# A transformer layer on one core: w_down opens in its seven-product form instead of with four plain jobs

## The chip, the cores and the metric

The kernel runs on one core of one Trainium2 chip. The metric is device time in microseconds (us) of one execution, the median of several runs. Work is spread over TensorE (PE, matrix products), VectorE (DVE), ScalarE (ACT), GpSimd (POOL, which here mostly issues transfers) and SyncE (SP, which issues most loads). Each engine takes its own instructions strictly in the order in which the program lists them, and engines wait for one another by semaphores.

## The reference, cut to what matters

A hybrid encoder layer on a sequence of 512 tokens of width 2048. The part that the change touches is the last product of the feed-forward half:

```
h = rmsnorm(x, ffn_norm_w)
x = x + (silu(h @ w_gate) * (h @ w_up)) @ w_down     # w_gate, w_up: 2048 x 5632; w_down: 5632 x 2048
return rmsnorm(x, final_norm_w)
```

Ahead of it stand an RMSNorm, a projection `w_in`, dilated attention and gated linear attention, and the projection `w_out`. All data is fp32.

## The kernel before, in words

*Split products.* An fp32 operand is split into a high part (a cast to fp32r on ACT) and a low part (the difference, a subtraction on VectorE). A product is then three matmuls: high by high, high by low, low by high.

*Seven-product form.* A 2 x 2 block product is done with seven block products instead of eight, at the price of sums of blocks ahead of it and sums of products behind it (Strassen's way, in Winograd's form). The operands of the seven are called B11, B21, B22 (single blocks) and T1 to T4 (sums). The gate and up projections (`Feed`, "gate/up") are done so: 44 units, gate and up in turn, each of four pieces and with seven PSUM banks. `sums` makes the block sums of the weights on VectorE (L1493 to L1495), `split` the casts on ACT (L1506) and the differences on VectorE (L1511), `products` the matmuls (L1589, L1603). At a unit's end `evac7` empties its seven banks: nine copies on ACT (from L1629), adds on VectorE (L1623, L1624), and additions done by transfers that POOL issues (L1648 to L1655). `finish` applies the gate (SiLU, and the product of gate and up, L1697) and POOL stores the result to DRAM, `gd` (L1699).

*Pre-made sums.* VectorE has little to do in the w_out stage, so `ff.ahead()` makes there the block sums of 21 pieces of gate/up and stores them in DRAM; gate/up later only loads these (`self.pre`). They are the second piece of every other unit from the third on.

*w_down.* Its 44 tiles of 128 rows (k-tiles) are done in three parts. First come four plain jobs on k-tiles 0 to 3, one for each 512 columns: 4 half pieces of weights by 4 banks of 128 tokens by 3 matmuls each (L346 to L348). Their weights come through the stream `st` (loads L209, casts L237, differences L218), their operand from `gd` through `g_load` (L1816) and `g_split` (L1824 to L1828), and `evac_down` scales a bank on ACT and has POOL add it into `xd` in DRAM. Then `Down([[2, 4], [6, 8], [10, 12], [14, 16]])` does k-tiles 4 to 35 in the seven-product form. A number there names a duo: two tiles of `gd` (a "pair operand" each, two k-tiles), four k-tiles. A list of duos is a chunk, whose seven products stay in PSUM while its duos are added up; then they are copied out and added to partial products in DRAM, `md`. `run` takes steps in the order chunk, column half (C), product (ORDER), duo, 12 matmuls each (L2023 to L2025). Per step one block of weights (1024 elements per partition) is cast (L1991), and its difference taken (L1999), two steps ahead; T1, T3 and T2 first need a sum (L1976, L1979). `operands()` makes a pair operand from `gd`: load (L1917), four adds of 256 (L1931 to L1934), then casts and differences of four parts, B11 (256 wide), F2, T13 and T24 (512 wide; L1943 to L1947). It is a generator; `dn.make(n)` takes n steps of it. Last come four plain jobs on k-tiles 36 to 39 and a finish on 40 to 43.

*The hand-over.* During the last gate/up unit `down_start(q)` runs after each piece q. It loads the first operands of w_down and splits them. The first plain job makes Down's operands beside its matmuls (`before_down`).

*Order and buffers.* The order of the code is the order in every engine's queue. There are 8 PSUM banks (`ps`), 33 wide slots of SBUF (`b`, 1024 elements per partition) and 36 narrow ones (`a`, 512). A load is issued by SP in its turn, once its slot is free, and SP waits there until it is.

Of the kernel before, what the change touches and what calls it, by code (L numbers as in the profile page):

```python
# [36 lines left out]
KEEP_X, KEEP_F, MOST_4 = 5, 2, 13  # L37
# [81 lines left out]
def layer(nc, tc, x, attn_norm_w, w_in, rel_table, gw_f, gb_f, gw_b, gb_b, gla_norm_w, w_out,  # L119
# [7 lines left out]
    with tc.manual_schedule(), \  # L127
# [1389 lines left out]
        class Feed(Blocks):  # L1517
# [10 lines left out]
            def __init__(self):  # L1528
# [7 lines left out]
                    i for i, (u, q) in enumerate(seq) if u > 1 and q == 1 and u % 2 == 0)}  # L1536
# [295 lines left out]
        def down_start(q):  # L1832
            if q == 0:
                g_load(0)
            if q == 1:
                st.until = down_pieces
                st.limit = 3
                st.load()
                g_load(1)
            if q == 2:  # L1840
                g_split(0)
                st.split(down_first + 2)
            if q == 3:
                dn.make(1)
# [4 lines left out]

        def evac_down(c):  # L1850

            def f(banks):
                for t in range(4):
                    y = s2.get()
                    act.activation(y.t, banks[t].t, AF.Copy, scale=rstd2[:, t:t + 1])
                    put(banks[t])
                    pool.dma_start(out=xd[4 * c + t], in_=y.t, accum_op=OP.add)
                    put(y)
            return f

        def before_down(c):
            def f(i):
                if c == 0 and i == 0:
                    g_split(1)
                dn.make(1)
                if c == 2 and i >= 2 or c == 3:
                    dn.load()
                if c == 3 and i >= 2:
                    dn.prime(i - 2)
            return f  # L1870
# [6 lines left out]
        class Down:  # L1877

            ORDER = ((0, 1, "B11"), (6, 2, "T4"), (1, 3, "B21"), (3, None, "T1"), (4, None, "T3"), (2, None, "T2"),
# [4 lines left out]
            def __init__(self, chunks):  # L1884
# [14 lines left out]
            def load(self):  # L1899
                while self.todo and len(self.raw) < 8 and s4.free:  # L1900
# [7 lines left out]
            def operands(self):  # L1908
# [5 lines left out]
                def load():  # L1914
                    if qs and len(s4.free) > 1 and len(raws) < 2:
                        r = s4.get(F32, [P, 2, 512])
                        sp.dma_start(out=r.t.rearrange("p f t -> p (f t)"), in_=gd[qs[0]])  # L1917
                        raws.append((qs.popleft(), r))

                load()  # L1920
                load()
                yield
                while raws or qs:
                    load()
                    if not raws or len(s2.free) + 2 * (MOST_4 - state["big"]) < 9 + 1 or len(s2.free) < 4:
                        yield
                        continue
                    q, r = raws.popleft()
# [5 lines left out]
                    tt(t24.t[:, z], t24.t[:, a], f2[:, a], op=OP.subtract)  # L1934
                    yield
                    todo, slots = [], {}
                    for name, src, n in (("B11", n1[:, a], 256), ("F2", f2, 512), ("T13", t13.t, 512),
                                         ("T24", t24.t, 512)):
                        slots[name], hi, lo, hf = half_split(src, n)
                        todo.append((src, hi, lo, hf))  # L1940
                    for i, (src, hi, lo, hf) in enumerate(todo):
                        if i == 0:
                            act.activation(hi, src, AF.Copy, scale=-1.0)  # L1943
                            dve.scalar_tensor_tensor(lo, src, -1.0, hf, op0=OP.mult, op1=OP.subtract)
                        else:
                            act.copy(hi, src)
                            tt(lo, src, hf, op=OP.subtract)  # L1947
                        if i:
                            put((r, t13, t24)[i - 1])
                        if i == 1:  # L1950
                            load()
                        if i % 2:
                            yield
                    (_, b1h, b1l, _), (_, f2h, f2l, _), (_, t13h, t13l, _), (_, t24h, t24l, _) = todo
                    self.x[q] = dict(slots=slots, B11=(b1h, b1l), B21=(f2h[:, a], f2l[:, a]),
                                     B22=(f2h[:, z], f2l[:, z]), T1=(t13h[:, a], t13l[:, a]),
                                     T3=(t13h[:, z], t13l[:, z]), T2=(t24h[:, a], t24l[:, a]),
                                     T4=(t24h[:, z], t24l[:, z]))
# [154 lines left out]
            def run(self):  # L2113
                n_last = len(self.seq) - 14
                for i, (ch, C, k, d) in enumerate(self.seq):
# [16 lines left out]
                    while q not in self.x or q + 1 not in self.x:  # L2132
                        self.make(1)
# [4 lines left out]
                    if i % 14 in (0, 1, 2, 5, 11, 12, 13):  # L2138
                        self.make(1)
# [46 lines left out]
        down_first = len(st.halves)  # L2186
        for c in range(4):
            j = job("B", [piece512(w_down, c * 512, k) for k in (0, 2)], list(range(4)),
                    lambda k: gT[k], evac_down(c), before=before_down(c))
            if c == 3:  # L2190
                j.drop = drop_g
# [151 lines left out]
```

## Time and profile before

| | |
|---|---|
| median of 3 runs | 2139.51 us (2138.58 to 2139.54) |
| the profiled execution | 2140.3 us, its span 2138.5 us, granted TensorE clock 0.999 |
| PE matmul, busy | 2126.0 us, 99% of the span |
| DVE busy | 1826.6 us, 85% |
| ACT busy | 1264.8 us, 59% |
| POOL busy | 388.7 us, 18% |
| costliest lines | L1603 and L1589, gate/up's matmuls; L1506 and L1511, its casts and differences |

Busy time is the time in which an engine has an instruction in work; the chain of waits follows the work that ended last from the end of the span back to its start. In the rows of a timeline stand start (us), duration, engine, line, operation, the tile written and the tiles read, and in brackets the idle time before it with what ended it. In a row of a stretch stand its length, busy time (and instructions) of PE, PE's weight loads, DVE, ACT and POOL, the granted clock of TensorE, the mean share of the transfer engines and GB/s. A row of transfers gives their count, size and median us from issue to landing.

### The profile page before, as it was taken

The page shows a single profiled execution, that of the slowest core. Times are in us where ns is not written, and L with a number is a line of the kernel's source. Part 1 is how long each engine was busy: PE and PEld are TensorE (multiplying, and loading weights), DVE is VectorE, ACT ScalarE, POOL GpSimd, SP SyncE. Part 2 cuts the span into 40 slices and gives each one's busy share as a digit, 9 for nine tenths or more (in the row PEclk, how much of TensorE's full clock was granted, in tenths as well). Part 3 has the DMA queues.
Part 4 walks back from the last instruction along what each step waited for, and adds up shares of the span by engine and source line. Part 5 has one row for each costly group of instructions (what it writes and reads, how often), then busy time and mean ns, then how long its engine had stood idle before and what let it go on. Part 6 is the DMA issues. An engine that isn't in the chain of part 4 may idle for free.

```text
span 2138.5 us, 32543 instructions
## 1 busy us (share of the span) xinstructions
PE 2126.0 (99%) x11410; PEld 1825.3 (85%) x11410; DVE 1826.6 (85%) x3002; ACT 1264.8 (59%) x2281; POOL 388.7 (18%) x531
## 2 busy tenths in 40 slices
PE   9999999999999999999999999999999999999998
PEld 7888888888888889888888888888888888888887
DVE  5699999888878788899899898998999888887885
ACT  8445555477776546455555555555555666666762
POOL 0011121332222010011221122112121220332000
PEclk9999999999999999999999999999999999999999
DMA  6367777877676773477767777677667897999572
GB/s 205 128 184 181 180 180 184 203 219 212 189 228 209 244 253 108 140 177 183 190 174 184 185 180 186 178 179 196 176 181 187 247 277 248 201 255 249 188 249 79
DMA packets 272369, 416.85 MB, mean 195 GB/s; under 512 B 19853, under 2 KB 164477, under 8 KB 272206
## 3 DMA queue, kind: packets, MB, share of 16 engines
q1 hardware_dynamic: 208926, 280.10, 40.9%
q0 software_dynamic: 62960, 134.15, 29.4%
q8 instruction: 90, 1.47, 0.3%
q14 instruction: 73, 0.60, 0.1%
q10 hardware_dynamic: 320, 0.53, 0.1%
HBM read 289.57 MB, written 71.93 MB: 169 GB/s over the span
## 4 chain that ended last, share of the span: by engine, by line
PE 56%; DVE 1%; DMA 1%; ACT 1%; issue 0%; SPq 0%; DVEq 0%; ACTq 0%
PE ps L1603 25%; PE ps L1589 13%; PE ps L2024 5%; PE ps L2023 5%; PE ps L2025 5%; PE ps L347 1%; PE ps L348 1%; PE ps L346 1%; PE ps L2240 1%; PE ps L2239 1%; PE ps L2238 1%; DMA a<-xd 0%; DMA gd<-b 0%; ACT b L237 0%; DVE a L1847 0%
## 5 line engine op out<-in xcount | busy, mean ns | idle before, releaser
L1506 ACT CAST b<-b 128x1024 fp32r<-128x1024 f32 (+1 forms) x473 | 433.7, 945 | 293.5 <-DVE b L1511 199.9
L1603 PE MATMUL ps<-b,b 128*128 128x512 f32 x1760 | 517.2, 393 | 0.4 <-ACT b L1506 0.2
L1511 DVE TENSOR_TENSOR b<-b,b 128x1024 fp32r<-128x1024 f32 (+1 forms) x473 | 495.7, 1084 | 18.8 <-ACT b L1506 8.9
L1603 PE MATMUL ps<-a,b 128*128 128x512 f32 x1488 | 436.4, 393 | 0.6 <-DVE b L1623 0.6
L1603 PEld LDWEIGHTS ps<-b,b 128*128 128x128 f32 x1760 | 298.1, 188 | 33.2 <-ACT b L1506 0.7
L1589 PEld LDWEIGHTS ps<-b,b 128*128 128x128 f32 x1760 | 289.9, 190 | 42.4
L1589 PE MATMUL ps<-b,b 128*128 128x256 f32 x1760 | 318.0, 280 | 0.0
L1589 PEld LDWEIGHTS ps<-a,b 128*128 128x128 f32 x1488 | 246.6, 189 | 39.2 <-DVE b L1511 0.5
L1603 PEld LDWEIGHTS ps<-a,b 128*128 128x128 f32 x1488 | 248.9, 188 | 25.7 <-ACT b L1506 0.8
L1589 PE MATMUL ps<-a,b 128*128 128x256 f32 x1488 | 267.5, 280 | 0.1
L1999 DVE TENSOR_TENSOR b<-b,b 128x1024 fp32r<-128x1024 f32 x112 | 136.5, 1221 | 31.8 <-ACT b L1991 30.0
L1493 DVE TENSOR_TENSOR b<-b 128x512 f32<-128x512 f32 x212 | 145.2, 685 | 2.4 <-DMA grd<-b 0.9
L346 PE MATMUL ps<-b,b 128*128 128x512 f32 x332 | 134.8, 406 | 0.0
L1991 ACT CAST b<-b 128x1024 fp32r<-128x1024 f32 x112 | 116.6, 1052 | 30.1 <-DVE b L1979 16.4
L348 PE MATMUL ps<-b,b 128*128 128x512 f32 x332 | 130.0, 392 | 0.0
L347 PE MATMUL ps<-b,b 128*128 128x512 f32 x332 | 129.9, 391 | 0.0
L1648 POOL DMA_DIRECT2D b<-a x58 | 50.2, 866 | 413.2 <-ACT b L1506 272.1
L1654 POOL DMA_DIRECT2D b<-a x58 | 50.1, 864 | 285.9 <-DMA b<-a 160.9
L1494 DVE TENSOR_TENSOR b<-b,b 128x256 f32<-128x256 f32 x212 | 90.1, 425 | 7.4
L1495 DVE TENSOR_TENSOR b<-b,b 128x256 f32<-128x256 f32 x212 | 90.2, 425 | 7.3
L218 DVE TENSOR_TENSOR b<-b,b 128x512 fp32r<-128x512 f32 x116 | 77.0, 685 | 20.7 <-ACT b L237 20.5
L1629 ACT COPY a<-ps 128x256 f32<-128x256 f32 x58 | 21.6, 372 | 122.0 <-PE ps L1589 121.8
(313 smaller groups left out, 4215.5 us busy)
## 6 DMA issues: line engine op xcount, KB each, us to landing
b<-in_w_gate_dram SPq DMA_DIRECT2D x109, 512.0 KB, 4.0
b<-in_w_in_dram SPq DMA_DIRECT2D x94, 512.0 KB, 4.0
b<-in_w_up_dram SPq DMA_DIRECT2D x88, 512.0 KB, 3.9
b<-in_w_down_dram SPq DMA_DIRECT2D x88, 512.0 KB, 8.0
b<-a POOLq DMA_DIRECT2D x174, 256.0 KB, 4.5
b<-in_w_out_dram SPq DMA_DIRECT2D x32, 512.0 KB, 4.6
md<-a POOLq DMA_DIRECT2D x56, 256.0 KB, 6.9
gd<-b POOLq DMA_DIRECT2D x22, 512.0 KB, 3.9
```

The source lines that it names most:

```text
L346: mm(o, xh.t[:, c], wh.t[:, w], start=first and not on, stop=False, skip_group_check=on)
L347: mm(o, xh.t[:, c], wl.t[:, w], start=False, stop=False, skip_group_check=on)
L348: mm(o, xl.t[:, c], wh.t[:, w], start=False, stop=last, skip_group_check=on)
L1493: dve.tensor_tensor(s_[:, :, 0:2], r[:, :, 1:3], r[:, :, 0:1].to_broadcast(shape), op=OP.add)
L1506: act.copy(o, src)
L1511: dve.tensor_tensor(o, src, h, op=OP.subtract)
L1589: mm(o, wl, xh, start=False, stop=end, skip_group_check=True)
L1603: mm(o.rearrange("p (s t) -> p s t", s=2), wh, x_, start=first and p == 0, stop=False, skip_group_check=True)
L1991: act.copy(hi.t, self.src[i].t)
L1999: dve.tensor_tensor(lo.t, s.t, hi.f, op=OP.subtract)
L2023: mm(o, xh[:, t], wh, start=new and j == 0, stop=False, skip_group_check=True)
L2024: mm(o, xh[:, t], wl, start=False, stop=False, skip_group_check=True)
```

## The change

The four plain jobs go, with `evac_down`, `before_down` and their loads. Down takes k-tiles 0 to 3 as well, and its chunks become `[[0, 2], [4, 6, 8], [10, 12], [14, 16]]`: 4, 6, 4 and 4 pair operands. `down_start` now loads weight blocks, casts the first two (`prime`) and makes parts of the first chunk's pair operands during the last unit. For that `operands()` does the first chunk's four pair operands part by part, first B11 and F2 of each (`raw_parts`), which need no sum, then sums and T24, then T13. ORDER takes the plain blocks first (B11, B21, then T4), and blocks of weights are loaded in that order. The 21 pre-made sums of gate/up are other ones: all eight pieces of the last two units, and the second piece of every third unit. MOST_4 (how many wide slots may hold narrow operands) falls from 13 to 10.

```diff
-KEEP_X, KEEP_F, MOST_4 = 5, 2, 13
+KEEP_X, KEEP_F, MOST_4 = 5, 2, 10
...
-                    i for i, (u, q) in enumerate(seq) if u > 1 and q == 1 and u % 2 == 0)}
+                    i for i, (u, q) in enumerate(seq)
+                    if u >= len(self.units) - 2 or u > 1 and q == 1 and u % 3 == 1)}
...
         def down_start(q):
             if q == 0:
-                g_load(0)
+                dn.make(1)
             if q == 1:
-                st.until = down_pieces
-                st.limit = 3
-                st.load()
-                g_load(1)
+                dn.load()
+                dn.make(2)
             if q == 2:
-                g_split(0)
-                st.split(down_first + 2)
+                dn.load()
+                dn.prime(0)
+                dn.make(2)
             if q == 3:
-                dn.make(1)
+                dn.load()
+                dn.prime(1)
+                dn.make(2)
...
-            ORDER = ((0, 1, "B11"), (6, 2, "T4"), (1, 3, "B21"), (3, None, "T1"), (4, None, "T3"), (2, None, "T2"),
+            ORDER = ((0, 1, "B11"), (1, 3, "B21"), (6, 2, "T4"), (3, None, "T1"), (4, None, "T3"), (2, None, "T2"),
                      (5, None, "B22"))
...
-                                  for blk in (1, 2, 3, 0) for d in range(len(duos)))
+                                  for blk in (1, 3, 2, 0) for d in range(len(duos)))
...
-                while self.todo and len(self.raw) < 8 and s4.free:
+                while self.todo and len(self.raw) < 4 * len(self.chunks[self.todo[0][0]]) and s4.free:
...
+                n_first = 2 * len(self.chunks[0])
+                first = []
+                load(2)
+                yield
+                while len(first) < n_first:
+                    load(2)
+                    if not raws or not room():
+                        yield
+                        continue
+                    q, r = raws.popleft()
+                    raw_parts(q, r)
+                    first.append((q, r))
                     yield
+                load(1)
+                rest = []
+                for q, r in first:
+                    t13, t24 = sums(r)
+                    put(r)
+                    sum_parts(q, t13, t24, ("T24",))
+                    rest.append((q, t13, t24))
+                    yield
+                for q, t13, t24 in rest:
+                    sum_parts(q, t13, t24, ("T13",))
+                    yield
...
-                    if i % 14 in (0, 1, 2, 5, 11, 12, 13):
+                    if C or i % 2:
                         self.make(1)
...
-        for c in range(4):
-            j = job("B", [piece512(w_down, c * 512, k) for k in (0, 2)], list(range(4)),
-                    lambda k: gT[k], evac_down(c), before=before_down(c))
...
-        dn = Down([[2, 4], [6, 8], [10, 12], [14, 16]])
+        dn = Down([[0, 2], [4, 6, 8], [10, 12], [14, 16]])
```

Three queues at the hand-over show what moves. In their rows stand the line (of the kernel in question), the operation, the tile written (numbered) and the tiles read, and the size.

SP before, from the load of the first pair operand of w_down's second g tile on (`b_1859` to `b_1861` and `b_1871` are pieces of the plain jobs' weights; L1816 and L1917 load from `gd`):

```order
L1816 DMA b_1853_17729<-gd 128x1024
L209 DMA b_1859_17776<-in_w_down_dram 128x2x512
L209 DMA b_1860_17778<-in_w_down_dram 128x2x512
L209 DMA b_1861_17780<-in_w_down_dram 128x2x512
L1816 DMA b_1862_17782<-gd 128x1024
L209 DMA b_1871_17832<-in_w_down_dram 128x2x512
L1917 DMA b_1872_17862<-gd 128x1024
L1917 DMA b_1873_17864<-gd 128x1024
L1917 DMA b_1881_17927<-gd 128x1024
```

SP after, at the same place (L1897 loads from `gd`, L1886 blocks of w_down; these eight are all that the first chunk's first column half needs; `b_1855`, `b_1869` and `b_1877` are the second, third and fourth pair operand):

```order
L1897 DMA b_1855_17735<-gd 128x1024
L1886 DMA b_1860_17778<-in_w_down_dram 128x2x512
L1886 DMA b_1861_17780<-in_w_down_dram 128x2x512
L1886 DMA b_1862_17782<-in_w_down_dram 128x2x512
L1886 DMA b_1863_17784<-in_w_down_dram 128x2x512
L1886 DMA b_1864_17786<-in_w_down_dram 128x2x512
L1886 DMA b_1865_17788<-in_w_down_dram 128x2x512
L1886 DMA b_1866_17790<-in_w_down_dram 128x2x512
L1886 DMA b_1867_17792<-in_w_down_dram 128x2x512
L1897 DMA b_1869_17800<-gd 128x1024
L1897 DMA b_1877_17848<-gd 128x1024
```

Where three loads of weights stood between two of `gd`, eight stand now, and two of `gd` behind them.

ACT before, from the last casts of gate/up's weights (L1506) to the first copy out of the last unit's first bank, `ps_710`:

```order
L1506 CAST b_1864_17785<-b_1854_17736 128x1024
L1824 ACTIVATE b_1867_17820<-b_1853_17729 128x512
L1827 CAST b_1868_17823<-b_1853_17729 128x512
L237 CAST b_1869_17826<-b_1859_17776 128x512
L237 CAST b_1870_17829<-b_1859_17776 128x512
L1629 COPY a_790_17867<-ps_710_17694 128x256
```

ACT after, the same stretch (L1908 and L1911 are parts of pair operands, L2011 casts of blocks of w_down; `a_795` and `a_797` are T24 of the first two pair operands, sums that VectorE makes):

```order
L1506 CAST b_1872_17809<-b_1853_17696 128x1024
L2011 CAST b_1875_17844<-b_1860_17778 128x1024
L1908 ACTIVATE a_792_17850<-b_1869_17800 128x256
L1911 CAST b_1878_17853<-b_1869_17800 128x512
L1908 ACTIVATE a_793_17858<-b_1877_17848 128x256
L1911 CAST b_1880_17861<-b_1877_17848 128x512
L2011 CAST b_1881_17892<-b_1861_17780 128x1024
L1911 CAST b_1883_17902<-a_795_17897 128x512
L1911 CAST b_1884_17911<-a_797_17906 128x512
L1630 COPY a_798_17915<-ps_710_17698 128x256
```

Ahead of the bank's first copy stand now the parts of the third and fourth pair operand (`b_1869`, `b_1877`), a block of weights, and two sums of VectorE.

VectorE before, at the last unit's first two adds and behind them (L1825 and L1828 are the plain jobs' operand, L1931 to L1934 a pair operand's sums):

```order
L1623 TENSOR_TENSOR a_790_17867<-a_790_17867,ps_710_17694 128x256
L1624 TENSOR_TENSOR a_790_17867<-a_790_17867,ps_711_17699 128x256 x2
L1623 TENSOR_TENSOR a_791_17868<-ps_712_17704,a_790_17867 128x256
L1623 TENSOR_TENSOR a_791_17868<-ps_713_17709,a_790_17867 128x256
L1623 TENSOR_TENSOR b_1874_17866<-ps_712_17704,a_791_17868 128x256
L1623 TENSOR_TENSOR b_1874_17866<-ps_714_17714,a_790_17867 128x256
L1825 SCALAR_TENSOR_TENSOR b_1875_17892<-b_1862_17782,b_1875_17892 128x512
```

VectorE after, ahead of the same add (now L1624; `b_1854` and `b_1855` are the first two pair operands):

```order
L1912 TENSOR_TENSOR b_1880_17861<-b_1877_17848,b_1880_17861 128x512
L2019 TENSOR_TENSOR b_1882_17894<-b_1861_17780,b_1881_17892 128x1024
L1927 TENSOR_TENSOR a_794_17896<-b_1854_17733 128x256
L1928 TENSOR_TENSOR a_794_17896<-b_1854_17733 128x256
L1929 TENSOR_TENSOR a_795_17897<-b_1854_17733,a_794_17896 128x256
L1930 TENSOR_TENSOR a_795_17897<-a_795_17897,b_1854_17733 128x256
L1912 TENSOR_TENSOR b_1883_17902<-a_795_17897,b_1883_17902 128x512
L1927 TENSOR_TENSOR a_796_17905<-b_1855_17735 128x256
L1928 TENSOR_TENSOR a_796_17905<-b_1855_17735 128x256
L1929 TENSOR_TENSOR a_797_17906<-b_1855_17735,a_796_17905 128x256
L1930 TENSOR_TENSOR a_797_17906<-a_797_17906,b_1855_17735 128x256
L1912 TENSOR_TENSOR b_1884_17911<-a_797_17906,b_1884_17911 128x512
```

The sums of the first two pair operands stand directly ahead of the bank's add, and behind the fourth pair operand's difference (`b_1877`), where before the add came first and the operands' sums behind it.

More of the change, by code (lines that the diff above doesn't have):

```diff
@@ L1848, in residual @@
             put(bank)
[L1850 to L1870, printed above, removed]
         def drop_g(k):
@@ L1912, in operands, with load @@
                 raws = deque()
-                def load():
-                    if qs and len(s4.free) > 1 and len(raws) < 2:
+                def load(most):
+                    while qs and len(s4.free) > 3 and len(raws) < most:
                         r = s4.get(F32, [P, 2, 512])
@@ L1918, in load, with room, parts, raw_parts @@
                         raws.append((qs.popleft(), r))
[L1920 to L1928, printed above, removed]
+                def room():
+                    return len(s2.free) + 2 * (MOST_4 - state["big"]) >= 9 + 1 and len(s2.free) >= 4
+                def parts(todo, names):
+                    for n in names:
+                        src, w = todo[n]
+                        slots, hi, lo, hf = half_split(src, w)
+                        if n == "B11":
+                            act.activation(hi, src, AF.Copy, scale=-1.0)
+                            dve.scalar_tensor_tensor(lo, src, -1.0, hf, op0=OP.mult, op1=OP.subtract)
+                        else:
+                            act.copy(hi, src)
+                            tt(lo, src, hf, op=OP.subtract)
+                        yield n, slots, hi, lo
+                def raw_parts(q, r):
+                    x_ = self.x[q] = {"slots": {}}
+                    for n, slots, hi, lo in parts({"B11": (r.t[:, 1, a], 256), "F2": (r.t[:, 0], 512)}, ("B11", "F2")):
+                        x_["slots"][n] = slots
+                        if n == "B11":
+                            x_["B11"] = (hi, lo)
+                        else:
+                            x_["B21"], x_["B22"] = (hi[:, a], lo[:, a]), (hi[:, z], lo[:, z])
+                def sums(r):
                     n1, f2 = r.t[:, 1], r.t[:, 0]
@@ L1954, in operands, with sum_parts @@
[L1954 to L1958, printed above, removed]
+                    return t13, t24
+                def sum_parts(q, t13, t24, names):
+                    x_ = self.x[q]
+                    for n, slots, hi, lo in parts({"T13": (t13.t, 512), "T24": (t24.t, 512)}, names):
+                        x_["slots"][n] = slots
+                        i, j = ("T1", "T3") if n == "T13" else ("T2", "T4")
+                        x_[i], x_[j] = (hi[:, a], lo[:, a]), (hi[:, z], lo[:, z])
+                        put(t13 if n == "T13" else t24)
@@ new lines, in operands @@
+                for q, r in first:
[7 more added lines that the diff above has]
+                    yield
+                while raws or qs:
+                    load(2)
+                    if not raws or not room():
+                        yield
+                        continue
+                    q, r = raws.popleft()
+                    t13, t24 = sums(r)
+                    yield
+                    raw_parts(q, r)
+                    put(r)
+                    load(2)
+                    yield
+                    sum_parts(q, t13, t24, ("T13", "T24"))
+                    yield
```

25 lines of the change are left out of this document (2 added, 23 removed).

## The prediction

> **What bounds the kernel now.** I read the page first, then TensorE's waits, then the stretch in which gate/up hands over to w_down, engine by engine.
>
> ```profile
> span 2138.5 us, 32543 instructions
> PE 2126.0 (99%) x11410; PEld 1825.3 (85%) x11410; DVE 1826.6 (85%) x3002; ACT 1264.8 (59%) x2281; POOL 388.7 (18%) x531
> ...
> PE ps L1188 <- DVE warm L436: 1.1, 1, 1.1
> PE ps L1603 <- DVE b L1623: 0.8, 2, 0.6
> PE ps L347 <- DVE b L218: 0.6, 1, 0.6
> ```
>
> TensorE is busy in 2126.0 of 2138.5 us, and its longest wait for anything after the start is 0.6 us. Whatever removes matmuls shortens the kernel by their issue interval, and whatever makes TensorE wait lengthens it one for one. The duration of a matmul overlaps the next one, so the interval is what counts. Here it is in the plain jobs that the change removes (the first row, and one 78 matmuls later) and in the seven-product form that takes their place (the first row, and one 9 later):
>
> ```profile
> 1693.91 0.40 PE L346 MATMUL ps<-b,b 128*128 128x512 f32 x1
> ...
> 1711.60 0.39 PE L346 MATMUL ps<-b,b 128*128 128x512 f32 x1
> ...
> 1737.44 0.39 PE L2023 MATMUL ps<-b,a 128*128 128x512 f32 x1
> ...
> 1739.48 0.39 PE L2023 MATMUL ps<-b,a 128*128 128x512 f32 x1
> ```
>
> 17.69 us by 78 and 2.04 by 9 both give 0.227 us. Plain jobs begin at 1693.9, and Down at 1737.4: these 43.5 us are also when ACT and VectorE make Down's first operands. That cover is what the change takes away.
>
> **The change, part by part.**
>
> *Matmuls.* Four plain jobs of 48 (4 half pieces, 4 banks, 3 matmuls) go: 192. One more duo in Down costs 2 column halves, 7 products, 12 matmuls each: 168. 24 fewer by 0.227 us: **-5.4 us**, all on the path.
>
> *Block sums in gate/up.* Units 2 to 41 lose 7 of 20 pre-made sums, and the last two units get 7 more. A sum is the three adds in the rows below, 1618.21 less 1616.69, so 1.52 us; seven are 10.6 us on VectorE, and that much more of the kernel if nothing hid them.
>
> ```profile
> 1612.34 0.42 DVE L1623 TENSOR_TENSOR a<-a,ps 128x256 f32<-128x256 f32 x1 [1.37 <-ACT a L1629]
> ...
> 1616.69 0.69 DVE L1493 TENSOR_TENSOR b<-b 128x512 f32<-128x512 f32 x1
> ...
> 1618.21 2.08 DVE L1511 TENSOR_TENSOR b<-b,b 128x768 fp32r<-128x768 f32 x2
> ...
> 1633.50 0.85 DVE L1623 TENSOR_TENSOR a<-ps,a 128x256 f32<-128x256 f32 x2 [0.27 <-PE ps L1589]
> ...
> 1636.19 0.69 DVE L1493 TENSOR_TENSOR b<-b 128x512 f32<-128x512 f32 x1
> ```
>
> The unit from 1616.69 to 1636.19 has no pre-made sum, takes VectorE 19.5 us, exactly one unit of TensorE, and still holds a wait for TensorE of 0.27; the unit before it had one and idles 1.37. Two bare units in a row thus still fit: cost 0, hidden under gate/up's matmuls. The count of pre-made sums stays 21, so the w_out stage only reads other weights: 0.
>
> *Evictions and transfers.* The 16 scaled copies and 16 adding stores of the plain jobs go; Down has four chunks as before, so its evictions stay the same in number. Neither ACT nor POOL holds TensorE here: 0. The smaller limit on wide slots moves operands between two pools: 0.
>
> *The opening wait.* Now the stretch where it is decided. The last unit's seven banks are emptied by copies on ACT and adds on VectorE; the first product of w_down takes the one free bank and then the first of those seven, after 3 matmuls, 0.68 us in, at 1694.6. Before, nothing stood ahead of that emptying:
>
> ```profile
> 1689.93 0.37 ACT L1629 COPY a<-ps 128x256 f32<-128x256 f32 x1 [4.44 <-PE ps L1589]
> 1690.34 0.42 DVE L1623 TENSOR_TENSOR a<-a,ps 128x256 f32<-128x256 f32 x1 [2.95 <-ACT a L1629]
> ```
>
> ACT had waited 4.44 us for TensorE, and the bank was free at 1690.8. Now the raw parts of four pair operands, two weight splits and two T24 parts stand ahead of it on both engines, and the third and fourth pair operand come by transfers that SP issues behind eight loads of w_down. When do these land? SP's queue and the store that its second load must wait for:
>
> ```profile
> 1675.57 0.56 POOL L1699 DMA_DIRECT2D gd<-b  x1 [7.17 <-DVE b L1697]
> 1679.93 3.47 ACT L1506 CAST b<-b 128x768 fp32r<-128x768 f32 x4 [3.00 <-DMA gd<-b]
> ...
> 1678.78 1.82 SPq L209 DMA_DIRECT2D b<-in_w_down_dram  x3
> 1680.66 0.46 SPq L1816 DMA_DIRECT2D b<-gd  x1
> 1684.12 0.37 SPq L209 DMA_DIRECT2D b<-in_w_down_dram  x1
> 1684.58 1.57 SPq L1917 DMA_DIRECT2D b<-gd  x3
> ...
> 1680.00:1684.00 4.00, 4.00 (x25) 3.56 (x24) 3.93 (x6) 4.00 (x6) 1.72 (x2) 1.00 0.74 208
> 1684.00:1688.00 4.00, 4.00 (x23) 3.43 (x22) 3.39 (x5) 1.49 (x3) 0.00 (x0) 1.00 1.03 297
> 1688.00:1692.00 4.00, 4.00 (x27) 3.64 (x27) 1.26 (x3) 1.02 (x3) 0.00 (x0) 1.00 1.07 347
> 1692.00:1696.00 4.00, 4.00 (x22) 3.37 (x22) 2.28 (x6) 3.28 (x9) 1.75 (x2) 1.00 1.02 411
> 1696.00:1700.00 4.00, 4.00 (x19) 3.34 (x18) 3.97 (x10) 3.83 (x8) 0.00 (x0) 1.00 1.10 297
> ...
> b<-in_w_down_dram SPq DMA_DIRECT2D x8, 512.0 KB, 10.8
> b<-gd SPq DMA_DIRECT2D x6, 512.0 KB, 10.6
> ...
> DMA to landing us min/median/max: 4.2/5.6/11.0
> ```
>
> The slot of SP's second gd load is the source of that store, which landed at 1679.9 (ACT waited for it). So from 1680.0 SP issues one gd load, eight of w_down and two more of gd: 11 of 0.524 MB, 5.8 MB, beside some 0.5 MB that POOL adds into SBUF. From 1680 on there was always more queued than moved; the last column (GB/s) by 4 us gives 0.83, 1.19, 1.39, 1.64 and 1.19 MB, 6.24 in all by 1700. The fourth pair operand lands at about **1700**. A second way to it: in before, the third gd load was issued at about 1685 behind some six other loads and took about 11 us (the last row is for all 16 loads of L1917); three more ahead of it at the 1.5 us that each of seven then took give 1700.5. The ends: at the mean of the first two rows, 253 GB/s, 6.3 MB take 25 us, 1705; at the 411 of the fourth from 1682 on, 15 us, 1697. And if a gd load could overtake the rest, its slot would still have to be free, which TensorE sees to with the unit's second piece, half of a 19.5 us unit before 1693.9; with the least landing of 4.2 that is 1688.
>
> Weighed against a rule: the Trainium skill, "DMA: Bandwidth & Descriptors", section on queues, rings and completion order, says that an engine consumes the descriptors of a ring in their order; by it the two loads cannot overtake, and the sum is that with 1700. The trace leans that way: gd loads here took 10.6 us.
>
> From this landing to the bank: ACT casts 256 and 512 wide, then a weight cast; VectorE a 1024 subtraction, then twice four adds and, each after an ACT cast, a 512 subtraction, then the bank's add. Durations:
>
> ```profile
> 1739.99 1.05 ACT L1991 CAST b<-b 128x1024 fp32r<-128x1024 f32 x1
> 1749.90 1.22 DVE L1999 TENSOR_TENSOR b<-b,b 128x1024 fp32r<-128x1024 f32 x1
> 1751.04 1.22 DVE L1976 TENSOR_TENSOR b<-b,b 128x1024 f32<-128x1024 f32 x1
> ...
> 1696.53 0.42 DVE L1931 TENSOR_TENSOR a<-b 128x256 f32<-128x256 f32 x1
> 1697.99 0.69 DVE L218 TENSOR_TENSOR b<-b,b 128x512 fp32r<-128x512 f32 x1
> 1698.60 0.42 DVE L1944 SCALAR_TENSOR_TENSOR a<-b,a 128x256 fp32r<-128x256 f32 x1
> 1695.17 0.62 ACT L1827 CAST b<-b 128x512 fp32r<-128x512 f32 x1
> ```
>
> Four adds take 1.46 (1696.53 to 1697.99), a 512 op 0.61, a 1024 op 1.14 from start to start. 0.8 (two casts from start to start) + 1.05 + 1.2 + 1.4 + 0.6 + 0.6 + 1.4 + 0.6 + 0.7 (the last subtraction and bank add's wait) + 0.4 = 8.8. The bank is free at 1708.8 and was wanted at 1694.6: **+14.2 us**. Bounds: +2 (landing at 1688) to +19 (1705).
>
> *VectorE's debt in the first products.* After that add VectorE still owes, before the eighth product step can begin: 6 adds of the last unit (6 by 0.42, 2.5), 8 weight subtractions, 5 weight sums and one gate multiply, 1024 wide (14 by 1.14, 16.0), two more four-add sums (2.9) and 7 operations 512 wide (7 by 0.61, 4.3): 25.7, and about 1 us of waits for ACT's casts in between. TensorE needs 9 + 6 by 12 = 81 matmuls, 18.4 us. It waits the difference: **+8.0 us** (7.3 without those waits, 9 with twice as much). What is late next? The other 20 steps of the first chunk, 54.4 us of TensorE, ask VectorE for 18 weight subtractions, 11 weight sums and a gate multiply (30 by 1.14, 34.2), and for parts of five pair operands: five four-add sums (7.3), five ops 256 wide (0.34 each without the start-up, 1.7) and 13 of 512 (7.9). That is 51.1, so VectorE keeps up with 3 us to spare: 0.
>
> *Clock.* A wait that long has a price of its own:
>
> ```profile
> 2130.00:2134.00 4.00, 0.37 (x4) 0.16 (x2) 3.62 (x12) 1.18 (x6) 0.00 (x0) 1.00 0.04 13
> 2134.00:2138.50 4.50, 0.00 (x0) 0.00 (x0) 0.37 (x1) 0.00 (x0) 0.00 (x0) 0.51 0.60 223
> ```
>
> The last matmul ends in the first of these windows, at about 2130.4; in the second the granted clock is 0.51, so idle time lowers it, and the same may hold here. After the 14 us wait TensorE would start cold, but there it has VectorE's debt to wait for anyway; after the second wait some of it shows. Bounds: 0, and 3.7 (two cold starts that each last the 3.7 us from 2130.4 to the second window, at half speed, 1.85 lost in each). I take **+1**.
>
> The Trainium skill, "TensorE: Matmul & The Clock Gate", Part 1 (the HAM clock gate), says that after an idle window of about 3.4 us the array runs at half clock until about 3.4 us of work have passed. The trace agrees with the first half (0.51); by the rule each exposed cold start costs about 1.7 us (an estimate from that page), which would make the sum 0.7 longer.
>
> *Sum.* The profiled execution took 2140.3 us, 0.8 above the median. 2140.3 - 5.4 + 14.2 + 8.0 + 1.0 = 2158.1, so **2157.3** against the median of 2139.5. Its own range, with the landing at 1697 to 1705 and the ends of debt and clock: 2139.5 - 5.4 + 11.2 + 7.3 = 2153 to 2139.5 - 5.4 + 19 + 9 + 3.7 = 2166.
>
> **The rivals.**
>
> *The loads land in time, the debt stays.* If the third and fourth operand are in SBUF by 1687, the bank is free when it is wanted; VectorE's own work then ends a little after TensorE's, and the debt of 7.3 to 8 us remains: 2139.5 - 5.4 + 7.7 = 2141.8. For it: the least time of a gd load is 4.2 us, and the median 5.6. Against: eight loads stand ahead. It decides at a landing before 1688.
>
> *All is hidden.* If VectorE is further ahead than its row count lets me think (its 7 sums less in the last two units are 10.6 us, more than the debt), only the matmuls show: 2134.1, faster. The place is VectorE's queue between 1674 and 1694; it decides where all that stands ahead of the bank's add is done by 1694.2. Against: that work needs the loads, and VectorE can't use time that it has before its data is there.
>
> *A later shortage.* The three-duo chunk wants 12 weight blocks and 6 pair operands made during the first chunk, and stores of partial products share SP's queue with loads. If a load is late at the second chunk by one round of 10.8 us, the time is 2168.
>
> **How the numbers follow.** Forecast (waits at the opening and debt) 0.70, loads in time 0.13, all hidden 0.07, later shortage on top 0.10. The range from 2141 to 2167 holds the first, most of the second and the near part of the last. 0.2%, 4.3 us, is about what a measurement of this kernel can tell from no change: faster is under 2135.2 (the hidden case and a little), the same up to 2143.8 (loads in time), slower the rest: 0.08, 0.12, 0.80.
>
> **What would show it.** Right: TensorE waits once for 12 to 16 us for a VectorE add of the last unit (or ACT's copy) near 1695, after 3 matmuls of Down; ACT waits there for a gd load; then two or three waits of 1 to 5 us for 512-wide operand subtractions; all else in the chain stays TensorE; granted clock below 1 only there. Wrong: no wait over 1 us at 1695 means that the transfers came in time; waits in units 2 to 41 would mean that the bare units don't fit; a wait at the second chunk's first product would be the last rival. The step I trust least is the landing at 1700.

## The result and the profile after

The changed kernel takes 2170.22 us (2169.59 to 2172.73, 4 runs) against 2139.53: 1.0146 times the time before, with a 95% interval of 1.0129 to 1.0164. It is slower, as forecast, but by 31 us and not by 18, and beyond the forecast's range, which ended at 2167.

The page of the kernel after (span, busy time of the engines):

```profile
span 2168.5 us, 32438 instructions
PE 2131.5 (98%) x11386; PEld 1824.0 (84%) x11386; DVE 1844.0 (85%) x3020; ACT 1261.2 (58%) x2267; POOL 374.5 (17%) x515
```

TensorE has 24 matmuls less and is nevertheless busy 5.5 us longer: some of its time passes at the slow clock, as the rows of stretches below show. Its waits in the stretch from 1640 to 1800 us (total, times, longest):

```profile
PE ps L2043 <- DVE a L1624: 15.9, 1, 15.9
PE ps L2044 <- DVE b L2019: 3.1, 7, 0.8
PE ps L2045 <- DVE b L1912: 2.8, 2, 2.2
PE ps L1604 <- ACT b L1506: 1.0, 1, 1.0
PE ps L2043 <- ACT b L2011: 0.9, 1, 0.9
PE ps L1590 <- DVE b L1511: 0.5, 2, 0.3
```

The first row is the wait that was forecast, for VectorE's add that empties the last unit's bank, after three matmuls of Down. The third row is the forecast debt (operand parts). The second and fifth are new: most of their waits lie 30 us later. On the engines, TensorE first, the places look like this:

```profile
1689.67 0.73 PE L1604 MATMUL ps<-a,b 128*128 128x512 f32 x2 [0.98 <-ACT b L1506]
...
1697.67 0.39 PE L2045 MATMUL ps<-b,a 128*128 128x512 f32 x1
1713.96 0.80 PE L2043 MATMUL ps<-b,a 128*128 128x512 f32 x1 [15.91 <-DVE a L1624]
...
1735.33 0.50 PE L2045 MATMUL ps<-b,b 128*128 128x512 f32 x1 [2.22 <-DVE b L1912]
...
1767.17 0.50 PE L2043 MATMUL ps<-b,b 128*128 128x512 f32 x1 [0.88 <-ACT b L2011]
...
1800.49 0.50 PE L2044 MATMUL ps<-b,b 128*128 128x512 f32 x1 [0.38 <-DVE b L2019]
```

ACT, whose brackets tell when transfers landed:

```profile
1687.96 0.42 ACT L1908 ACTIVATE a<-b 128x256 fp32r<-128x256 f32 x1 [5.34 <-DMA b<-gd]
...
1688.79 1.78 ACT L1506 CAST b<-b 128x768 fp32r<-128x768 f32 x2
...
1703.53 0.42 ACT L1908 ACTIVATE a<-b 128x256 fp32r<-128x256 f32 x1 [12.01 <-DMA b<-gd]
...
1704.72 0.42 ACT L1908 ACTIVATE a<-b 128x256 fp32r<-128x256 f32 x1 [0.26 <-DMA b<-gd]
...
1766.07 1.04 ACT L2011 CAST b<-b 128x1024 fp32r<-128x1024 f32 x1 [7.98 <-DMA gd<-b]
```

VectorE, SP and POOL:

```profile
1676.03 1.23 DVE L1698 TENSOR_TENSOR b<-b,b 128x1024 f32<-128x1024 f32 x1 [2.40 <-DMA b<-a]
...
1703.98 0.42 DVE L1909 SCALAR_TENSOR_TENSOR a<-b,a 128x256 fp32r<-128x256 f32 x1 [11.02 <-ACT a L1908]
...
1713.49 0.41 DVE L1624 TENSOR_TENSOR a<-a,ps 128x256 f32<-128x256 f32 x1
...
1767.15 1.22 DVE L2019 TENSOR_TENSOR b<-b,b 128x1024 fp32r<-128x1024 f32 x1 [6.00 <-ACT b L2011]
```

```profile
1677.29 6.11 SPq L1897 DMA_DIRECT2D b<-gd  x2
1683.51 7.40 SPq L1886 DMA_DIRECT2D b<-in_w_down_dram  x8
1691.01 3.97 SPq L1897 DMA_DIRECT2D b<-gd  x3
...
1747.39 5.37 SPq L1886 DMA_DIRECT2D b<-in_w_down_dram  x6
```

```profile
1677.56 0.56 POOL L1700 DMA_DIRECT2D gd<-b  x1 [6.96 <-DMA b<-sd]
...
1757.72 0.56 POOL L1700 DMA_DIRECT2D gd<-b  x1 [16.66 <-DVE b L1698]
```

ACT gets the third pair operand at 1703.5 and the fourth at 1704.7, and until then VectorE stands idle for 11.02 us. The bank's add runs at 1713.5. Later, from 1758 on, ACT waits 7.98 us for the landing of a store of gate/up, and VectorE 6.00 for ACT. The granted clock in the stretches that matter (the column behind POOL's):

```profile
1688.00:1692.00 4.00, 2.51 (x13) 1.44 (x12) 3.47 (x5) 3.52 (x5) 0.58 (x1) 0.97 0.97 286
1692.00:1696.00 4.00, 4.00 (x15) 3.53 (x16) 0.96 (x1) 0.00 (x0) 0.00 (x0) 0.60 1.10 291
...
1712.00:1716.00 4.00, 2.04 (x5) 1.65 (x6) 2.96 (x8) 3.76 (x11) 0.00 (x0) 0.50 0.00 0
1716.00:1720.00 4.00, 4.00 (x13) 3.15 (x12) 3.97 (x8) 1.21 (x2) 0.00 (x0) 0.61 0.00 0
...
1736.00:1740.00 4.00, 3.38 (x9) 2.20 (x8) 4.00 (x5) 2.88 (x5) 0.70 (x2) 0.52 1.03 266
1740.00:1744.00 4.00, 4.00 (x12) 2.72 (x11) 3.96 (x8) 0.50 (x2) 1.06 (x2) 0.63 1.06 301
```

A ledger can be made from the starts of all matmuls: whatever one starts later than 0.227 us after the one before it is lost. Down's first matmul starts at 1697.20 and not at 1693.91: 3.3 us lost in gate/up's last unit. Then 16.1 at the bank, 2.5 by the half clock behind it, 6.8 from 1730 to 1750 (about 3.4 of waits and 3.4 of half clock), and 7.1 from 1764 to 1801, in pieces of about a microsecond. Beyond that there is no loss. 35.8 less the 5.4 of the matmuls removed is 30.4; the span grew by 30.0.

### The profile page after: what moved, and what is told of

Its sections match the earlier page's. It is cut to its first block, busy times and chain, and to the rows that moved or that the text cites. A ratio compares the mean times of both kernels' runs of the same rounds, so it can differ in the third digit from the quotient of the medians.

```text
span 2168.5 us, 32438 instructions
## 1 busy us (share of the span) xinstructions
PE 2131.5 (98%) x11386; PEld 1824.0 (84%) x11386; DVE 1844.0 (85%) x3020; ACT 1261.2 (58%) x2267; POOL 374.5 (17%) x515
## 4 chain that ended last, share of the span: by engine, by line
PE 54%; DVE 2%; DMA 2%; ACT 1%; issue 1%; SPq 0%; DVEq 0%; ACTq 0%
PE ps L1604 24%; PE ps L1590 12%; PE ps L2045 5%; PE ps L2044 5%; PE ps L2043 5%; DMA b<-gd 1%; PE ps L2254 1%; PE ps L2253 1%; PE ps L2252 1%; DVE b L2019 1%; DMA gd<-b 1%; PE ps L347 0%; PE ps L348 0%; PE ps L346 0%; DVE b L1999 0%
## 5 line engine op out<-in xcount | busy, mean ns | idle before, releaser
L1506 ACT CAST b<-b 128x1024 fp32r<-128x1024 f32 (+1 forms) x473 | 433.9, 945 | 298.5 <-DVE b L1511 208.2
L1604 PE MATMUL ps<-b,b 128*128 128x512 f32 x1760 | 517.3, 393 | 0.4 <-ACT b L1506 0.2
L2019 DVE TENSOR_TENSOR b<-b,b 128x1024 fp32r<-128x1024 f32 x126 | 152.8, 1220 | 46.0 <-ACT b L2011 43.9
L2011 ACT CAST b<-b 128x1024 fp32r<-128x1024 f32 x126 | 131.3, 1054 | 46.5 <-DVE b L1999 23.5
L2043 PE MATMUL ps<-b,a 128*128 128x512 f32 x296 | 116.8, 395 | 15.9 <-DVE a L1624 15.9
L346 PE MATMUL ps<-b,b 128*128 128x512 f32 x316 | 128.3, 406 | 0.3 <-DVE b L477 0.3
L347 PE MATMUL ps<-b,b 128*128 128x512 f32 x316 | 123.7, 391 | 0.5 <-DVE b L218 0.3
L348 PE MATMUL ps<-b,b 128*128 128x512 f32 x316 | 123.7, 391 | 0.2 <-DVE b L464 0.2
L2044 PE MATMUL ps<-b,a 128*128 128x512 f32 x296 | 116.8, 395 | 0.6 <-DVE b L2019 0.6
L2045 PE MATMUL ps<-b,a 128*128 128x512 f32 x296 | 116.7, 394 | 0.0
L1494 DVE TENSOR_TENSOR b<-b,b 128x256 f32<-128x256 f32 x212 | 90.2, 425 | 7.4
```

The costliest lines, as they stand in the source:

```text
L346: mm(o, xh.t[:, c], wh.t[:, w], start=first and not on, stop=False, skip_group_check=on)
L347: mm(o, xh.t[:, c], wl.t[:, w], start=False, stop=False, skip_group_check=on)
L1506: act.copy(o, src)
L1604: mm(o.rearrange("p (s t) -> p s t", s=2), wh, x_, start=first and p == 0, stop=False, skip_group_check=True)
L2011: act.copy(hi.t, self.src[i].t)
L2019: dve.tensor_tensor(lo.t, s.t, hi.f, op=OP.subtract)
```

## The experiments

Three theories on the opening were to be told apart. **A**, late data: the restart at 1714 hangs on the landing of the fourth operand and VectorE's work behind it. **B**, queue place: the bank's copies simply stand behind too many operand parts. **C**: what gate/up's last unit loses adds to the rest. Times are to be read against 2170.2 after and 2139.9 before (the medians of the kernel before in these comparisons lay between 2139.7 and 2140.1).

**The g loads first**

```diff
-                load(2)
+                load(n_first)
                 yield
                 while len(first) < n_first:
-                    load(2)
```

> Against the changed kernel only SP's order differs: all four g loads of the first chunk are issued in the last unit's first quarter, ahead of the eight loads of w_down, and not two of them behind. Theory A (late data: TensorE's restart at 1714 is set by the landing of the fourth pair operand at 1704.7 and the 9.3 us chain behind it, VectorE stands idle from 1693 to 1704 and never makes it up): the fourth operand lands at 1690 to 1692, the first weight block at about 1692.5 sets the chain instead, the bank is free at about 1703.5, the restart comes 10 us earlier, and the time is 2160 (2154 to 2163). Theory B (queue place: the bank's copies and adds simply stand behind too many operand parts): the parts are as many as before, so at most the wait for data in their midst goes; 2165 or more.

2161.04 us, a gain of 9.2. ACT's rows:

```profile
1692.61 1.05 ACT L2010 CAST b<-b 128x1024 fp32r<-128x1024 f32 x1 [1.93 <-DMA b<-in_w_down_dram]
...
1703.18 0.37 ACT L1630 COPY a<-ps 128x256 f32<-128x256 f32 x1
```

ACT no longer waits there for the third and fourth operand but for the first weight block, until 1692.6 (and 0.64 us more for the second), and the bank's copy starts at 1703.2 instead of 1712.8. The operand parts on the queues are as many as before, and their data is earlier: theory A, and in its size.

**The bank's copies and adds ahead of the second weight split and the T24 parts**

```diff
-                        down_start(q)
                     done = None
                     if q == self.per - 1:
                         done = (self.evac7 if u > 1 else self.evac)(u, banks.pop(u))
...
+                    if u == len(self.units) - 1:
+                        down_start(q)
```

> Against the changed kernel only the place of the last unit's bank copies and adds differs: they stand ahead of the second weight split and the two T24 parts (the raw parts of the third and fourth operand still stand ahead). Theory A: the bank is free some 7 us earlier, at about 1706.5, but VectorE has the same work to do before the eighth product step, so what the first wait loses comes back as waits for operand parts: 2170 (2167 to 2171). Theory B: the 7 us are gained: 2163.

2169.81 us. The four largest of TensorE's waits from 1640 to 1900:

```profile
PE ps L2044 <- DVE a L1624: 9.7, 1, 9.7
PE ps L2045 <- DVE b L2020: 4.2, 9, 0.8
PE ps L2044 <- ACT b L1912: 3.0, 2, 2.7
PE ps L2044 <- ACT b L2012: 3.0, 2, 1.9
```

The first wait is 6.2 us shorter, and Down's waits for ACT of 6.0, which were 0.9, have come in its place. ACT's casts of the operand sums wait in their turn for VectorE's adds, 2.2 to 3.2 us each. So the work on the operands behind the data decides, not its order: theory A against B.

**The second operand's raw parts behind gate/up's last casts**

```diff
             if q == 1:
                 dn.load()
-                dn.make(2)
+                dn.make(1)
             if q == 2:
                 dn.load()
+                dn.make(1)
                 dn.prime(0)
```

> Against the changed kernel the raw parts of the second pair operand stand behind the last unit's last weight casts and not ahead of them. Theory A: gate/up ends 3.3 us earlier (TensorE's wait for ACT at 1689 and the cold clock behind it go), but TensorE's restart at 1714 hangs on the fourth operand's landing and not on this, so the opening wait grows by as much: 2170 (2168.5 to 2171). Rival C (the 3.3 us that gate/up's last unit lost add to the rest): 2167.

2169.64 us. Gate/up ends on time, and this row of TensorE's waits shows where that went:

```profile
PE ps L2044 <- DVE a L1624: 20.0, 1, 20.0
```

20.0 us instead of 15.9: TensorE would have waited through the 3.3 us lost in gate/up's last unit anyway. Rival C is out.

**The other choice of pre-made sums alone, in the kernel before**

```diff
-                    i for i, (u, q) in enumerate(seq) if u > 1 and q == 1 and u % 2 == 0)}
+                    i for i, (u, q) in enumerate(seq)
+                    if u >= len(self.units) - 2 or u > 1 and q == 1 and u % 3 == 1)}
```

> The kernel before with only the other choice of pre-made sums (all pieces of the last two units, and every third unit's second piece). Theory A: nothing of the 30 us comes from the bare units or from the eight more loads of sums as such; 2139.5, within 2 us. Rival D (two bare units in a row, or the loads of sums in the last units, hold TensorE): 2143 or more, with waits for weight differences in gate/up.

2142.42 us, 1.0012 times the time before (1.0003 to 1.0021, so 0.6 to 4.5 us): between theory A and rival D, a little more than the one allowed and a little less than the other asked for. TensorE's longest wait, ACT and POOL in the profiled execution, which at 2144.98 us was the longest of ten, so that its waits are above the typical ones:

```profile
PE ps L1604 <- ACT b L1506: 3.1, 2, 2.9
```

```profile
1686.44 3.46 ACT L1506 CAST b<-b 128x768 fp32r<-128x768 f32 x4 [9.41 <-DMA gd<-b]
```

```profile
1679.10 0.56 POOL L1700 DMA_DIRECT2D gd<-b  x1 [7.96 <-DMA b<-sd]
```

No wait of units 2 to 41 is among the longer ones, so the bare units fit. But the other half of rival D, the loads of sums in the last units, is seen in kind: in the last unit ACT waits 9.41 us, for a slot that the store of the unit before still reads. That store is issued at 1679.1 and not, as before, at 1675.6, and the two last units hold seven loads of sums more. In the changed kernel it is issued at 1677.6; there VectorE's product ahead of it had waited 2.40 us for POOL's adding transfers (the row of L1698), which took 6.5 us from issue to landing where they took 4.6 before.

**TensorE kept warm in the opening wait**

```diff
                 q = self.chunks[ch][d]
+                if i == 0:
+                    xh, xl = self.x[q][name]
+                    for _ in range(68):
+                        mm(self.banks[0].t, xh[:, 0:P], hi.t[:, 0], start=True, stop=True, skip_group_check=True)
```

> The changed kernel with 68 matmuls more, ahead of Down's first (they write its first bank, which the first real matmul starts afresh): at 0.227 us they fill 15.4 of the 16 us of the opening wait and keep the array warm. Theory A (from the landing on VectorE's work sets the times, TensorE's clock does not): the 2.5 us that the first matmuls lose at half clock go, but the wait for T13 parts at 1733 to 1738 grows by as much: 2170 (2168.5 to 2171). Rival E (the cold starts are a cost of their own, that adds): 2167.5 or less.

2170.18 us. The clock stays up until 1716 (first row), and yet the parts come no earlier. A cold stretch appears behind the restart (second row), after a wait of 1.9 us:

```profile
1712.00:1716.00 4.00, 2.11 (x10) 1.45 (x9) 3.18 (x8) 1.91 (x7) 0.00 (x0) 1.00 0.00 0
1716.00:1720.00 4.00, 4.00 (x11) 3.12 (x12) 3.75 (x8) 3.07 (x7) 0.00 (x0) 0.57 0.00 0
```

So the cold stretch was not taken away but moved by some microseconds, and whether a cold start costs anything of its own stays open. What the run shows: 15.4 us of additional matmuls in the wait cost nothing.

**The limit on loaded weight blocks**

```diff
-                while self.todo and len(self.raw) < 4 * len(self.chunks[self.todo[0][0]]) and s4.free:
+                while self.todo and len(self.raw) < 4 * len(self.chunks[self.now]) and s4.free:
```

(`self.now` is the chunk that runs.)

> The changed kernel with the limit on loaded weight blocks taken from the chunk that runs (8 in the first chunk), not from the chunk of the next load (12 as soon as the three-duo chunk is next). Theory F (the 7 us lost between 1764 and 1800 come from these early loads: they take the last free wide slots, so a weight cast gets the slot that the last store of gate/up still reads, and that store lands at 1765.9 behind the loads): the wait goes, 2163 (2162 to 2166). Rival G (VectorE has simply too much to do for the three-duo chunk's operands): 2168 or more, with the same waits for weight differences.

2161.28 us, a gain of 8.9. Down's waits from 1680 to 1810 are then these, and none of them is for a weight difference:

```profile
PE ps L2043 <- DVE a L1624: 17.1, 1, 17.1
PE ps L2045 <- DVE b L1912: 3.2, 2, 2.0
PE ps L2045 <- DVE a L1912: 1.2, 1, 1.2
```

Theory F holds, G is out. Read with this, the rows of the changed kernel say: the six early loads at 1747 took the last free wide slots, and the cast's next slot was the one that gate/up's last store, issued at 1757.7, read until it landed at 1765.9.

**Both edits**

> Both edits: the four g loads first, and the limit of 8 in the first chunk. If theory A and theory F each hold and the two losses are apart, the gains add: 2170.2 - 9.2 - 7 = 2154 (2152 to 2157). If one hides the other: 2158 or more.

2154.72 us: the two losses are for the most part apart. The gains by themselves would add to 18.1, and 15.5 came; 16.2 were expected, with the ledger's 7 us for the second.

**Slots turned, too**

```diff
             if q == 0:
+                s4.free.rotate(-2)
                 dn.make(1)
```

(With both edits, and with the bank's copies and adds first.)

> Besides both edits the bank copies and adds stand ahead of the T24 parts, and the two wide slots that gate/up's second last stores release are used last, so that the second g load need not wait for a store's landing at 1682.9. Theory A: all four operands are in by 1687 and the first weight block by 1689, VectorE starts 5 us earlier, the opening wait is under 2 us, and what is left is VectorE's debt in the first products, 8 to 12 us: 2146 (2143 to 2150). If transfers were already as fast as they can be (rival H): 2153 or more.

2152.98 us (2150.14 to 2155.72), a miss by 7, near rival H. The operands were in earlier, the third at 1687.4 and the fourth at 1690.1 (1703.4 and 1704.7 in the changed kernel), but not all by 1687 as expected, and the first weight block was late:

```profile
1691.58 1.05 ACT L2012 CAST b<-b 128x1024 fp32r<-128x1024 f32 x1 [4.10 <-DMA b<-in_w_down_dram]
```

It came at 1691.6, not at 1689. Its load was issued 4.0 us earlier than in the run with only the g loads first (1681.0, not 1684.9) and its cast began 1.0 earlier: the transfers had been the bound there, not the slot. The opening wait is down to 1.5 us, and the debt shows in the waits behind it:

```profile
PE ps L2044 <- DVE a L1624: 1.5, 1, 1.5
```

**Sums on GpSimd** (on the version with the slots turned, as all that follows)

```diff
                 for q, r in first:
-                    t13, t24 = sums(r)
+                    t13, t24 = sums(r, pool.tensor_tensor)
```

> The last version with the four adds of each of the first chunk's four pair operands on GpSimd and not on VectorE. Theory A (what is left is VectorE's debt before the T13 parts, 16 us of waits and cold matmuls in the first products): VectorE is relieved of 4 times 1.46 us and of four waits of 0.7 for the casts that stood between sum and difference, 8.6 us, and the time falls to 2145 (2143 to 2148). Rival I: GpSimd is slower at it than TensorE's need, or slows VectorE, and the operands come no earlier: 2151 or more.

And with the weight sums of the first chunk's first column half (in `add`; there are eight) and the order of `down_start` changed as well:

```diff
                 dn.load()
-                dn.prime(0)
                 dn.make(2)
+                dn.prime(0)
...
-                tt = dve.tensor_tensor
+                tt = (dve if ch or C else pool).tensor_tensor
```

> In addition the six weight sums of the first column half go to GpSimd (6 times 1.14 us on VectorE), and the raw parts of the third and fourth operand stand ahead of the first weight block's cast (VectorE idled 3.9 us there). Theory A: the debt is nearly gone, 2138 (2135 to 2141), which would be as fast as the kernel before or a little faster. Rival I: GpSimd is now the late one: 2145 or more, with waits of ACT for GpSimd's sums.

2151.28 us (2150.45 to 2155.64), and 2167.46 us: rival I both times. The 1.7 us between the first and the version without GpSimd's adds are no gain shown, as the two versions' runs overlap. The first of the two, GpSimd, VectorE and a wait of ACT:

```profile
1697.78 0.78 POOL L1929 TENSOR_TENSOR a<-b 128x256 f32<-128x256 f32 x1 [6.69 <-issue]
...
1699.23 0.72 POOL L1931 TENSOR_TENSOR a<-b,a 128x256 f32<-128x256 f32 x1
...
1708.20 1.71 POOL L1929 TENSOR_TENSOR a<-b 128x256 f32<-128x256 f32 x1
```

```profile
1701.45 1.23 DVE L1914 TENSOR_TENSOR b<-a,b 128x512 fp32r<-128x512 f32 x1 [3.49 <-ACT b L1913]
...
1710.38 1.75 DVE L2020 TENSOR_TENSOR b<-b,b 128x1024 fp32r<-128x1024 f32 x1
```

```profile
ACT b L1913 <- POOL a L1932: 12.0, 4, 5.0
```

An add that takes VectorE 0.42 takes GpSimd 0.72, and up to 1.71 while VectorE is at work. VectorE's 512-wide difference takes 1.23 instead of 0.69, its 1024-wide one 1.75 instead of 1.22. The Trainium skill, "GPSIMD Engine Reference", section 1 (specifications), says that GpSimd's interfaces to SBUF are shared with VectorE, with contention where a VectorE instruction has two SBUF inputs. The trace agrees, for the differences that grew longer have two. The slower adds, the longer differences and GpSimd's first add, which came only after 6.69 us, all put the sums back, and ACT waited 12.0 us for them; what each of the three cost by itself was not measured.

**Sums left out**

```diff
                 for q, r in first:
-                    t13, t24 = sums(r)
-                    put(r)
-                    sum_parts(q, t13, t24, ("T24",))
+                    v = []
+                    for n in range(2):
+                        x_ = Slot()
+                        x_.t, x_.home = r.t[:, n], None
+                        v.append(x_)
+                    sum_parts(q, v[1], v[0], ("T24",))
...
```

> The version with the slots turned (g loads first, limit of 8, bank copies first), but the sixteen adds that make the first chunk's T13 and T24 are left out: their parts are taken from the raw halves of the g tile instead, so that VectorE has less to do and GpSimd does nothing more. Theory A (the rest is VectorE's debt): 4 times 1.46 us and four waits of 0.7 less, 2153 - 8.6 = 2144.5 (2142 to 2147). Rival J (after the data is there, something else sets the pace of the first products: ACT, or the loads of weight blocks): 2150 or more.

(`v` holds the two halves of the operand, in the place of the sums.) And in `add`, where `own` is false in the first chunk's first column half, with the same order of `down_start` as in the second version with GpSimd:

```diff
                 s, b = r(0), {4: 1, 2: 2, 5: 3}[n]
-                tt(s.t, s.t, r(b).t, op=OP.add)
+                if own:
+                    tt(s.t, s.t, r(b).t, op=OP.add)
...
```

> The same, and the eight weight sums of the first column half are left out as well (a block stands in for each sum), five of them ahead of the last T13 part, 5.7 us; and the raw parts of the third and fourth operand stand ahead of the first weight block's cast. Theory A: the debt is all but gone, 2137 (2134 to 2140), near the 2134.1 that 24 matmuls less would give. Rival J: 2145 or more.

2141.69 us, 1.0007 times the time before (0.9997 to 1.0016), and 2137.02 us, 0.9985 (0.9976 to 0.9995). TensorE's waits of the second, from 1680 to 1810:

```profile
PE ps L2055 <- DVE b L2030: 1.1, 2, 0.9
PE ps L2056 <- DVE a L1914: 0.4, 1, 0.4
```

The adds took 11.3 us with them, where 8.6 were forecast (where the other 2.7 come from was not followed up), and the weight sums together with the changed order 4.7 more. With 17.8 us less for VectorE in the first column half (four sums of 1.46, four pauses of 0.7, eight weight sums of 1.14) 1.5 us are left of the waits. They were VectorE's debt, and rival J is out. Both kernels leave sums out that the result needs, so they only say what a version would be worth that had them from elsewhere. Of the versions that compute everything, none beats the kernel before.

## Why the prediction was wrong, step by step

The mechanism was right: TensorE waits once, after three matmuls of Down, for the last unit's bank, since on ACT and VectorE the parts of operands stand ahead that come behind eight loads; then comes VectorE's debt. The opening wait was mis-sized, and two things that were put at 0 were not: the other choice of pre-made sums, and what comes late behind the debt.

- *Matmuls, -5.4.* The page has 24 fewer, and where none waits they start at the forecast interval. With VectorE relieved, the time is 3.1 us under that of the kernel before (2137.0 against 2140.1), with 1.5 us of waits left.
- *Opening wait.* The bank was to be free at 1708.8 and was at 1714.0. 4.7 of these 5.2 us are the landing: 1704.7, not 1700. The other 0.5 is the chain of parts behind it (9.3, forecast 8.8). SP's second load could start at 1682.9 and not at 1680.0, because the store that it waits for was issued 2.0 us later and took 5.4 us, 1.0 longer. The step that failed here is "The count of pre-made sums stays 21 [...]: 0". It was costed for the w_out stage alone. That eight pieces of sums are read in the last two units, where it was one, was not; alone in the kernel before, this cost 2.4 us and made the same store later. That it is the cause in the changed kernel too is inferred from that run; no run has the change without it. The rest of the landing's error is the pace: eleven loads took 21.8 us from there, not 20. The upper end of its bounds, 1705, did hold.
- *Order of the transfers.* By the rule of the Trainium skill that was weighed ("DMA: Bandwidth & Descriptors", queues, rings and completion order) descriptors are consumed in ring order, though a later one may finish its write before an earlier one. The trace agrees with the first: the two g loads behind the eight landed 12.4 and 11.5 us after their issue, the fourth operand when the transfer engines were about to fall idle.
- *Gate/up's last unit.* Its 3.3 us were not forecast: the second operand's raw parts stand on ACT ahead of gate/up's last casts and wait for a load until 1688. They cost nothing, since TensorE would have waited for the fourth operand in any case.
- *Debt and clock, 8.0 + 1.* Together 9.3 us, forecast 9.0, but about 3.4 of waits and 5.9 of half clock. (The debt's own terms, 25.7 + 1 - 18.4, give 8.3 and not 8.0.) Each term by itself missed, the clock's beyond its upper bound of 3.7, and that the sum holds is in part luck. A reason why one would make up for the other is that VectorE catches up while TensorE runs at half clock; no run tells the two apart. Nor was the clock below 1 only behind the opening wait, as the signs had it: it also fell in gate/up's last unit.
- *"What is late next? [...] 0".* This is the largest single miss: 7.1 us by the ledger, 8.9 by the edit that takes them away. It took both misses to leave the range: without this one the sum below would be 2162.8, without the 5.2 of the opening wait 2164.7. VectorE's 3 us to spare were counted as if its data were always there. The raised limit on loaded blocks stood in the diff, and no term was made for it: six loads ahead of their need took the last free slots, and the cast behind them had to wait 7.98 us for a store. The rival "a later shortage" named a late load at the second chunk; it was a late slot in the first.

The forecast, the landing, the chain of parts, debt and clock, and the late slot: 2157.3 + 4.7 + 0.5 + 0.3 + 7.1 = 2169.9; measured were 2170.2.

## What to carry to other kernels

Cover taken away is paid for by the engine that used it: here VectorE has, by the prediction's count, some 25 us of work to do before the eighth product step. Of what was tried, another order of its queue gained nothing, GpSimd's help gained nothing that is clear of the spread or lost 14 us, and matmuls that filled TensorE's wait changed nothing; only earlier data, a free slot in time, or less work did. Where loads stand in one queue, put those first that the longest chain hangs on: four loads ahead of eight instead of around them were worth 9 us. And a prefetch limit is a claim on buffers: ask what the slot that it takes would have been used for, and who waits if the only other one is still being read.

## What was not expected of the hardware

The granted clock fell to 0.60 from 1692 to 1696 behind waits that are short each (0.98, 0.26 and 0.25 us): in the 4 us before, TensorE had been busy for 2.51. In the run with the slots turned the clock stayed at 1.00 through three such stretches from 1692 to 1704, with TensorE busy for 2.63 to 2.75 of 4 us, so these runs put no sharp limit on it. And GpSimd stood 6.69 us ahead of its first add with nothing to wait for that the profile shows, and 6.55 in the other run that gave it adds.
